# Splitting two weight quads in one operation: a float32 decoder trunk on one core

## The chip, the cores and the metric

One core of one Trainium2 chip. The metric is the device time of one execution in microseconds (us), as the median of several runs; lower is better. Engines: TensorE (PE: matmuls; PEld: its weight loads), VectorE (DVE), ScalarE (ACT), GpSimd (POOL), SyncE (SP: issues the DMAs).

## The reference, cut to what matters

A two-layer decoder trunk on 256 tokens of width 2048, all in float32. The first layer mixes tokens by causal pooling and memory attention, the second by differential attention over shared keys and values and memory attention. After each mixer stands the feed-forward part, width 8192, where the change is:

```python
def squared_relu_mlp(h, w1, w2):
    z = jax.nn.relu(h @ w1)
    return (z * z) @ w2
...
        x = x + squared_relu_mlp(rms_norm(x, ffn_norm[i]), w_ff1[i], w_ff2[i])
```

## The kernel before, in words

**Precision.** Every float32 operand is split in two: `hi`, the value rounded to the type float32r by a cast, and `lo`, the rest, `x - hi`, again in float32r. A product of two operands is hi x hi + hi x lo + lo x hi, all summed in PSUM. The activations are kept as such pairs. The weights come from memory as plain float32 and are split on the chip, just before use.

**The weights' way (class `Feed`, class `Plan`).** The host lays out all weights as 725 rows of 128 x 1024, in the order of use. A row holds eight blocks of 128 x 128; four neighbouring blocks, 512 columns, are a **quad**, so a row is two quads. `Feed.load` (L125) issues one DMA a row on SyncE into one of four buffers `raw`. `Feed._split` (L159) makes the pair: line 164 casts on ScalarE into `hi_ring`, line 165 subtracts on VectorE into `lo_ring`. Both rings have **six slots** of 512 columns. `_slots(n)` hands out n neighbouring slots, the next in turn; where fewer than n are left before the end it starts again at slot 0 and the slots at the end are left out of that round. A slot is free again when the matmuls of its quad have been recorded (`used`, `free`), and its next cast then waits on the chip for the last matmul that reads it.

`Plan` records in a dry run which quads and slab pieces will be used, in order. `Feed.fill` (L210), called when a quad is first used, prepares all splits up to three pieces ahead (`AHEAD`); where no slot is free it stops and goes on at the next call. `Feed._prepare` (L172) prepares one piece. After recording, a scheduler puts the instructions of each engine in the order in which they are then issued; each engine keeps to its order.

**Matmuls with a quad (`a_part`).** A tile of 128 output columns takes 16 blocks. For two blocks at a time, two matmuls of 512 columns multiply `hi` with both parts of the activations, and two of 256 columns multiply `lo` with their high part. A quad is eight matmuls. `hi` and `lo` are the stationary operand: the wait for a split stands at the weight load. In the feed-forward parts the tile's bank is `x_bank`, of which there is one; ScalarE copies it out (line 739, the eviction) before the next tile may begin, and VectorE and ScalarE turn it into squared activations (`z`, and sums of blocks of z, `sit`) for an **up tile** (first matrix), or VectorE adds it to the residual for a **down tile** (second matrix, output columns 0 to 1023).

**Products (`slab_jobs`, `product`).** Columns 1024 to 2047 of the second matrix are computed by seven products of blocks instead of eight, into seven banks p1 to p7 (numbered p0 to p6 in the program). Each 256 x 1024 piece of that matrix is a **slab** of two rows. VectorE forms sums of its four blocks (lines 187 to 197), and the slab is split in four pieces: two slots (for p0 and p1), one (p2), two (p3, p4), two (p5, p6). A product is three matmuls of 512 columns, two with `hi` and one with `lo` (lines 813 to 815). Here `hi` and `lo` are the moving operand.

**The order around the change (`ffn`).** After four up tiles and the opening of the seven banks come 12 up tiles, then three rounds of 24 tiles (8 down, 16 up); with each tile go one or two pieces of a slab, six, nine or six product matmuls at a tile's beginning, a slab in three tiles. So three tiles take six weight rows and one slab. A last part (`last`) does the last eight down tiles and the rest of the slabs. Both layers do the same.

Of the kernel before, what the change touches and what calls it, by code (L numbers as in the profile page):

```python
# [10 lines left out]
F32 = mybir.dt.float32  # L11
# [43 lines left out]
class Plan:  # L55
# [7 lines left out]
    def __init__(self):  # L63
        self.entries = []
        self.npos = 0
        self.jobs = []
        self.slabs = []
# [37 lines left out]
class Feed:  # L105


    def __init__(self, tc, wst, wpool, rows, plan, dry):
        self.tc, self.nc, self.wst, self.wpool, self.rows = tc, tc.nc, wst, wpool, rows
        self.plan, self.dry = plan, dry  # L110
        self.pos = 0
        self.slab_no = 0
        self.lp = self.pp = 0
        self.raw = {}
        self.split = {}
        self.t1 = None
        self.behind = None
        self.gate = None
        if not dry:
            self.hi = wpool.tile([P, SLOTS * 512], F32R, name="hi_ring")  # L120
            self.lo = wpool.tile([P, SLOTS * 512], F32R, name="lo_ring")
            self.busy = [False] * SLOTS
            self.at = 0
# [48 lines left out]
    def _prepare(self, p):  # L172
        sub, add = self.nc.vector.tensor_sub, self.nc.vector.tensor_add
        self.load(self.plan.need[p] + 1 + LOADS)
        if p[0] == "N":
            r = ("N", p[1] // 2)
            c = p[1] % 2 * 512
            if not self._split(p, self.raw[r][:, c : c + 512], 1):
                return False
            if c:  # L180
                del self.raw[r]
            return True
        ra, rb = self.raw[("S", p[1], 0)], self.raw.get(("S", p[1], 1))
        t1 = self.t1[1 if p[1] % 32 > 28 else p[1] % 2]

        def both():
            t2 = rb[:, 0:512].unsqueeze(1).to_broadcast([P, 2, 512])
            two = ra.rearrange("p (a c) -> p a c", a=2)
            sub(two, t2, two)

        if p[0] in "KL":
            one = add(t1, ra[:, 0:512], rb[:, 0:512])
            if self.gate:

                self.order(one, self.gate)
                self.gate = None
            sub(rb[:, 0:512], t1, rb[:, 512:1024])
            if p[0] == "L":
                both()
            return True  # L200
        src, n = ((ra, 2), (t1, 1), (rb, 2), (ra, 2))[p[2]]
        if not self._split(p, src, n):
            return False
        if p[2] == 0 and ("K", p[1]) in self.plan.need:
            both()
        if p[2] == 3:
            del self.raw[("S", p[1], 0)], self.raw[("S", p[1], 1)]
        return True
# [68 lines left out]
def program(ctx, tc, plan, dry, xT, memT, par, lam, cst, wst, yT):  # L277
# [8 lines left out]
    feed = Feed(tc, wst, wp, tp, plan, dry)  # L286
# [10 lines left out]
    def tick():  # L297
        now[0] += 1
        for _, fn in sorted(pend.pop(now[0], []), key=lambda x: x[0]):
            fn()  # L300
# [9 lines left out]
    def mmt(name):  # L310
        return pp.tile([P, 512], F32, tag="mm", bufs=3, name=name)
# [403 lines left out]
    def ffn(l, xs, tags, done):  # L715
# [16 lines left out]
        r = []  # L732
# [40 lines left out]
        def up_tile(q, i, ps):  # L773
            a_part(ps, "w_ff1", l, q * NK + i, range(NK), xs)
            if not r:
                r.append(rstd_from("x"))
            y = evict(ps)

            def first():
                nc.vector.tensor_add(y[:, 0:T], y[:, 0:T], y[:, T : 2 * T])  # L780
                stt(y[:, 0:T], y[:, 0:T], 0.0, r[0], ALU.max, ALU.mult)

            at(1, first)
            at(3, lambda: nc.scalar.activation(stage[i % 8], y[:, 0:T], AF.Square))  # L784
            if q == 0 or i > 0:
                convert(i, 3)
# [19 lines left out]
        def bank():  # L806
            return pp.tile([P, 512], F32, tag="st", bufs=1, name="x_bank")

        def product(p, q, i, a, hi, lo):

            ps = banks[p]
            first, last = q == 0 and i == 0, q == 3 and i == 7
            nc.tensor.matmul(ps, a[1], hi, start=first, stop=False)  # L813
            nc.tensor.matmul(ps, a[0], hi, start=False, stop=False)  # L814
            nc.tensor.matmul(ps, a[0], lo, start=False, stop=last)  # L815

        def slab_jobs(q, i):
            k = q * NK + 2 * i
            n = feed.slab(
                [[("w_ff2", l, k, c, 4), ("w_ff2", l, k + 1, c, 4)] for c in (2, 3)]  # L820
            )

            def plain(c, t):
                return (
                    z[:, 2 * i + c, t * P : t * P + P],
                    z[:, 2 * i + c, T + t * P : T + t * P + P],
                )

            def summed(c):
                return sit[:, i, c * P : c * P + P], sit[:, i, 512 + c * P : 512 + c * P + P]  # L830

            sides = (
                ((0, lambda: plain(0, 0)), (1, lambda: plain(1, 0))),
                ((2, lambda: summed(0)),),
                ((3, lambda: summed(1)), (4, lambda: summed(3))),
                ((5, lambda: summed(2)), (6, lambda: plain(1, 1))),
            )

            def run(j):
                hi, lo = feed.job(n, j)  # L840
                for c, (p, a) in enumerate(sides[j]):
                    s = slice(512 * c, 512 * c + 512)
                    product(p, q, i, a(), hi[:, s], lo[:, s])
                feed.job_used(n, j)

            return run

        def open_banks():
            tags = (("mm", 3), ("mm", 3), ("mm", 3), ("s", 2), ("s", 2), ("o", 1), ("t", 1))
            for p, (tag, bufs) in enumerate(tags):  # L850
                banks.append(pp.tile([P, 512], F32, tag=tag, bufs=bufs, name=f"p{p}"))

        def finish_banks():

            p1, p2, p5, p6, p3, p7, p4 = banks
            low = tp.tile([P, 2, 512], F32, tag="rows", bufs=3, name="c_a")
            upp = tp.tile([P, 2, 512], F32, tag="rows", bufs=3, name="c_b")
            c11, c12 = upp[:, 0, :], upp[:, 1, :]
            u, v = low[:, 0, :], low[:, 1, :]
            add, sub = nc.vector.tensor_add, nc.vector.tensor_sub  # L860
            nc.scalar.copy(u, p1)
            nc.scalar.copy(v, p5)
            add(c11, u, p2)
            add(u, u, p6)
            sub(c12, v, u)
            add(u, u, p7)
            add(c12, c12, p3)
            sub(v, v, u)
            sub(u, u, p4)

            def turn(h):
                c = 8 + 2 * h
                t4 = pp.tile([P, 2, T], F32, tag="ot"[h % 2], bufs=1, name="ct")
                for e in range(2):
                    n = (2 * h + e) // 4
                    w = (2 * h + e) % 4 * P
                    for t, side in enumerate((upp, low)):
                        nc.tensor.transpose(t4[:, e, t * P : t * P + P], side[:, n, w : w + P], ident)
                nc.vector.tensor_add(resid[:, c : c + 2, :], resid[:, c : c + 2, :], t4)
                done(c)  # L880
                done(c + 1)

            for h in range(4):
                at(8 + h // 2 * 2, lambda h=h: turn(h))

        groups = ((0,), (1, 2), (3,))
        for i in range(4):
            up_tile(0, i, mmt("ff1"))
        open_banks()

        for t in range(12):
            if t % 3 == 0:
# [21 lines left out]
        )  # L914

        def last(q=3):
            jobs = [(i, j) for i in range(4, 8) for j in range(4)]
            now_at = []

            def some(n):  # L920
                for _ in range(n):
                    i, j = jobs.pop(0)
                    if j == 0:
                        now_at[:] = [slab_jobs(q, i)]
                    now_at[0](j)
                    tick()

            def between(n):
                return lambda b: some(ends[n][b // 4]) if b > 0 and b % 4 == 0 else None

            for n in range(8):
                if n < 6:
                    some(ends[n][0])
                if n == 5:
                    finish_banks()
                ps = bank() if n < 6 else mmt("ff2")
                down_tile(q, n, ps, between(n) if n < 6 else None)
# [79 lines left out]
    for i in range(2):  # L1017
        c = slice(2 * i, 2 * i + 2)
# [34 lines left out]
    for i in range(2):  # L1053
        c = slice(2 * i, 2 * i + 2)
# [183 lines left out]
    for t in range(2):  # L1238
        four = "p (h d) -> p h d"
        hi, v4 = mv1[:, t, :].rearrange(four, h=4), ps[t].rearrange(four, h=4)  # L1240
        split_rows(hi, mv1_lo[:, :, t, :], v4, mem_c[0][:, t : t + 1])
    for i in range(2):
        c = slice(2 * i, 2 * i + 2)
# [114 lines left out]
    for c in range(3):  # L1358
# [5 lines left out]
        for i in range(2):  # L1364
            j = 2 * c + i
# [119 lines left out]
```

## Time and profile before

| | |
|---|---|
| median of 3 runs | 2032.11 us (2031.99 to 2032.57) |
| the profiled execution: its own time, taken as its span | 2030.2 us |
| feed-forward of the first layer, about | 250 to 930 us of the span |
| feed-forward of the second layer, about | 1340 to 2020 us |
| three tiles with their slab | 21.4 us |

Page 1 of the profile gives each engine's busy time; page 4 follows the chain of work that ended last back from the end; page 5 lists groups of instructions as line, engine, operation, output<-inputs, shapes, count | busy us, mean ns of one | idle time in front and what ended it. In a timeline a row is start, duration, engine, line, operation, and in brackets the idle time in front with what released it; "x2" merges two in a row. A list of waits has the waiting line, the one waited for, total us, times and longest. A row of stretches gives the window, then busy us and (count) for PE, PEld, DVE, ACT and POOL, the granted clock of TensorE, the DMA share and GB/s.

### The profile page before, as it was taken

How to read it: one execution, taken by the hardware profiler on the slowest of the kernel's cores; microseconds unless marked ns; L12 is line 12 of the kernel's file. 1: busy time of each engine (PE TensorE's matmuls, PEld its weight loads, DVE VectorE, ACT ScalarE, POOL GpSimd, SP SyncE). 2: the span in 40 equal slices, each digit the busy share in tenths (PEclk: the TensorE clock that was granted, in tenths of full speed). 3: DMA queues.
4: the chain of work that ended last, by engine and by line, in shares of the span. 5: the costliest groups of instructions: out<-in, count | busy, mean ns of one | idle time of the engine just before them, and what ended most of it. 6: DMA issues, size and time to landing. Idle time of an engine off the chain costs nothing.

```text
span 2030.2 us, 32210 instructions
## 1 busy us (share of the span) xinstructions
PE 2025.3 (100%) x11022; PEld 1744.0 (86%) x11022; DVE 1718.6 (85%) x3233; ACT 1352.6 (67%) x2537; POOL 53.5 (3%) x67
## 2 busy tenths in 40 slices
PE   9999999999999999999999999999999999999999
PEld 8888888888888888888888888888888888888888
DVE  8888889889879978999765798989879978888997
ACT  7765577666656756678665698566657656766764
POOL 0001300000000000000000000310000000000000
PEclk9999999999999999999999999999999999999999
DMA  9566556555556565655565534555555555565564
GB/s 318 167 201 190 191 176 204 191 197 198 187 198 203 185 205 195 206 178 178 187 235 191 173 122 155 188 180 200 187 198 198 187 204 194 188 213 195 193 209 135
DMA packets 110470, 390.75 MB, mean 192 GB/s; under 512 B 12512, under 2 KB 15200, under 8 KB 110304
## 3 DMA queue, kind: packets, MB, share of 16 engines
q1 hardware_dynamic: 110160, 388.68, 57.2%
q8 instruction: 86, 1.41, 0.3%
q14 instruction: 80, 0.66, 0.1%
q10 hardware_dynamic: 144, 0.01, 0.0%
HBM read 386.54 MB, written 2.10 MB: 191 GB/s over the span
## 4 chain that ended last, share of the span: by engine, by line
PE 99%; ACT 0%; DVE 0%; issue 0%
PE x_bank L418 33%; PE x_bank L420 16%; PE wo L418 6%; PE p L813 5%; PE p L814 5%; PE p L815 5%; PE wo L420 3%; PE u L418 2%; PE ff L418 2%; PE u L420 1%; PE q L452 1%; PE q L454 1%; PE k L452 1%; PE q L453 1%; PE k L454 1%; PE v L454 1%
## 5 line engine op out<-in xcount | busy, mean ns | idle before, releaser
L164 ACT CAST hi_ring<-raw 128x512 fp32r<-128x512 f32 x1193 | 736.0, 620 | 510.8 <-PE x_bank L418 302.9
L165 DVE TENSOR_TENSOR lo_ring<-raw,hi_ring 128x512 fp32r<-128x512 f32 x1193 | 816.2, 694 | 189.0 <-ACT hi_ring L164 148.9
L418 PE MATMUL x_bank<-fx,hi_ring 128*128 128x512 f32 x1920 | 601.8, 395 | 0.0
L420 PEld LDWEIGHTS x_bank<-fx,lo_ring 128*128 128x128 f32 x1920 | 360.6, 188 | 84.0
L420 PE MATMUL x_bank<-fx,lo_ring 128*128 128x256 f32 x1920 | 377.1, 278 | 0.0
L418 PEld LDWEIGHTS x_bank<-fx,hi_ring 128*128 128x128 f32 x1920 | 301.3, 189 | 9.4
L418 PE MATMUL x_bank<-z,hi_ring 128*128 128x512 f32 x960 | 300.9, 395 | 0.0
L165 DVE TENSOR_TENSOR lo_ring<-slab,hi_ring 128x1024 fp32r<-128x1024 f32 x188 | 229.9, 1223 | 54.2 <-ACT hi_ring L164 53.5
L164 ACT CAST hi_ring<-slab 128x1024 fp32r<-128x1024 f32 x188 | 196.8, 1047 | 73.3 <-PE x_bank L418 37.8
L420 PEld LDWEIGHTS x_bank<-z,lo_ring 128*128 128x128 f32 x960 | 180.3, 188 | 41.9
L420 PE MATMUL x_bank<-z,lo_ring 128*128 128x256 f32 x960 | 188.6, 278 | 0.0
L418 PE MATMUL wo<-cat,hi_ring 128*128 128x512 f32 x512 | 161.8, 397 | 0.3 <-DVE rc L389 0.3
L418 PEld LDWEIGHTS x_bank<-z,hi_ring 128*128 128x128 f32 x960 | 151.8, 189 | 6.4 <-ACT room L739 0.4
L420 PEld LDWEIGHTS wo<-cat,lo_ring 128*128 128x128 f32 x512 | 95.9, 188 | 22.0
L739 ACT COPY room<-x_bank 128x512 f32<-128x512 f32 x180 | 104.8, 582 | 2.0 <-PE x_bank L420 2.0
L420 PE MATMUL wo<-cat,lo_ring 128*128 128x256 f32 x512 | 101.5, 279 | 0.0
L813 PE MATMUL p<-hi_ring,sit 128*128 128x512 f32 x256 | 100.4, 392 | 0.0
L814 PE MATMUL p<-hi_ring,sit 128*128 128x512 f32 x256 | 100.1, 391 | 0.0
L815 PE MATMUL p<-lo_ring,sit 128*128 128x512 f32 x256 | 99.6, 389 | 0.0
L784 ACT ACTIVATE room<-room 128x256 f32<-128x256 f32 x128 | 53.2, 416 | 42.1 <-DVE room L314 41.9
L418 PEld LDWEIGHTS wo<-cat,hi_ring 128*128 128x128 f32 x512 | 78.3, 189 | 1.1 <-ACT mq L606 0.5
L813 PE MATMUL p<-hi_ring,z 128*128 128x512 f32 x192 | 75.1, 391 | 0.0
(343 smaller groups left out, 3078.2 us busy)
## 6 DMA issues: line engine op xcount, KB each, us to landing
raw<-in_w SPq DMA_DIRECT2D x596, 512.0 KB, 3.7
slab<-in_w SPq DMA_DIRECT2D x124, 512.0 KB, 3.6
memraw<-in_mem SPq DMA_DIRECT2D x5, 512.0 KB, 3.8
resid<-in_x SPq DMA_DIRECT2D x8, 256.0 KB, 5.6
room<-in_w SPq DMA_DIRECT2D x4, 512.0 KB, 5.0
out_y<-resid SPq DMA_DIRECT2D x16, 128.0 KB, 1.9
memraw<-in_mem SPq DMA_DIRECT2D x5, 256.0 KB, 5.6
memraw<-in_mem SPq DMA_DIRECT2D x2, 128.0 KB, 3.6
```

The source lines that it names most:

```text
L164: self.last_cast = self.nc.scalar.copy(hi, src)
L165: low = self.nc.vector.tensor_sub(lo, src, hi.bitcast(F32))
L418: nc.tensor.matmul(ps, hi, xs[:, k, :], start=first and c == 0, stop=False)
L420: nc.tensor.matmul(ps[:, T : 2 * T], lo, xs[:, k, 0:T], start=False, stop=last and c == len(ks) - 1,)
L452: nc.tensor.matmul(ps[t], x[t][1], hi, start=k == 0, stop=False)
L453: nc.tensor.matmul(ps[t], x[t][0], hi, start=False, stop=False)
L454: nc.tensor.matmul(ps[t], x[t][0], lo, start=False, stop=k == NK - 1)
L739: nc.scalar.copy(x, ps)
L784: at(3, lambda: nc.scalar.activation(stage[i % 8], y[:, 0:T], AF.Square))
L813: nc.tensor.matmul(ps, a[1], hi, start=first, stop=False)
L814: nc.tensor.matmul(ps, a[0], hi, start=False, stop=False)
L815: nc.tensor.matmul(ps, a[0], lo, start=False, stop=last)
```

## The change

A flag `pairs` is set when the seven banks are open and cleared at the start of `last`. While it is set, `_prepare` splits both quads of a row at once: it takes two neighbouring slots, casts 1024 columns with one instruction on ScalarE (line 187 of the changed file) and subtracts 1024 columns with one on VectorE (line 188). Each quad is still used and freed by itself. Slab pieces, and weight rows elsewhere, are split as before.

```diff
@@ class Feed, __init__
         self.gate = None
+        self.pairs = False
...
@@ def _prepare(self, p)
         if p[0] == "N":
+            if p in self.split:
+                return True
             r = ("N", p[1] // 2)
             c = p[1] % 2 * 512
+            if c == 0 and self.pairs and ("N", p[1] + 1) in self.plan.need:
+                a = self._slots(2)
+                if a is None:
+                    return False
+                t = self.raw.pop(r)
+                hi, lo = self.hi[:, a * 512 : a * 512 + 1024], self.lo[:, a * 512 : a * 512 + 1024]
+                self.nc.scalar.copy(hi, t)
+                self.nc.vector.tensor_sub(lo, t, hi.bitcast(F32))
+                for j in range(2):
+                    s = slice(512 * j, 512 * j + 512)
+                    self.split[("N", p[1] + j)] = (hi[:, s], lo[:, s], range(a + j, a + j + 1))
+                return True
             if not self._split(p, self.raw[r][:, c : c + 512], 1):
                 return False
...
@@ def ffn
         open_banks()
+        feed.pairs = True
...
         def last(q=3):
+            feed.pairs = False
             jobs = [(i, j) for i in range(4, 8) for j in range(4)]
```

## The prediction

> **What bounds the kernel now.** I read the page first: busy shares, the clock line of the slices, and the chain that ended last.
>
> ```profile
> span 2030.2 us, 32210 instructions
> ...
> PE 2025.3 (100%) x11022; PEld 1744.0 (86%) x11022; DVE 1718.6 (85%) x3233; ACT 1352.6 (67%) x2537; POOL 53.5 (3%) x67
> ...
> PEclk9999999999999999999999999999999999999999
> ...
> PE 99%; ACT 0%; DVE 0%; issue 0%
> ```
>
> The chain runs on TensorE for 99% of the span, at full granted clock. A busy TensorE alone could hide slow matmuls, so the waits come next: who waits for the splits, and whether TensorE ever does.
>
> ```profile
> PEld x_bank L418 <- ACT room L739: 0.4, 2, 0.2
> ...
> PEld mk L445 <- ACT hi_ring L164: 0.3, 1, 0.3
> ```
>
> ```profile
> ACT hi_ring L164 <- PE x_bank L418: 343.8, 489, 2.0
> DVE lo_ring L165 <- ACT hi_ring L164: 203.2, 364, 1.9
> ```
>
> In the first two rows TensorE's weight loads wait for a split once, 0.3 us, at the start. In the other two the splits wait: ScalarE's cast 489 times for TensorE to give a slot of the ring back, VectorE's subtraction 364 times for the cast. So the splits run ahead of TensorE, and what holds them is the ring of six slots, not either engine. Time on ScalarE or VectorE is worth nothing here; how far ahead they run is worth everything.
>
> **What the change does to the engines.** The groups of operations give both shapes, since slabs are split 1024 wide already.
>
> ```profile
> L164 ACT CAST hi_ring<-raw 128x512 fp32r<-128x512 f32 x1193 | 736.0, 620 | 510.8 <-PE x_bank L418 302.9
> L165 DVE TENSOR_TENSOR lo_ring<-raw,hi_ring 128x512 fp32r<-128x512 f32 x1193 | 816.2, 694 | 189.0 <-ACT hi_ring L164 148.9
> ...
> L165 DVE TENSOR_TENSOR lo_ring<-slab,hi_ring 128x1024 fp32r<-128x1024 f32 x188 | 229.9, 1223 | 54.2 <-ACT hi_ring L164 53.5
> L164 ACT CAST hi_ring<-slab 128x1024 fp32r<-128x1024 f32 x188 | 196.8, 1047 | 73.3 <-PE x_bank L418 37.8
> ```
>
> The changed kernel has 334 casts and 334 subtractions fewer, so 334 pairs (167 a layer). A pair costs ScalarE 1047 ns instead of 2 x 620, VectorE 1223 instead of 2 x 694: 334 x 193 ns = 64 us and 334 x 165 ns = 55 us less busy. Both leave idle engines idler: I count 0.
>
> What it takes away is lead. A pair needs two free neighbouring slots; at slot 5 it skips to slot 0 and leaves one unused; the cast waits until both are given back; and the first quad is ready only after 1.05 + 1.22 us instead of 0.62 + 0.69. I followed each slot through the order of both kernels' instructions: the matmul time between the last read of a slot and the first read of its next contents. Before, the shortest is 3.7 us for the high part and most are 5.1 to 5.8. After, most row pairs have 3.0 to 4.4, and twice in every three slabs (64 us) come places with 0.9 to 1.9. Per layer, place B comes 9 times and place C 8 times: 18 and 16 in all. On SyncE's queue row and slab loads only change places with their neighbours; a row's load follows a pair's subtraction, still three rows (8 us of matmuls) ahead, so I count the DMAs at nothing.
>
> **The prices of one hand-over**, from the timeline. Cadence and release:
>
> ```profile
> 503.46 0.39 PE L815 MATMUL p<-lo_ring,sit 128*128 128x512 f32 x1
> 503.68 0.39 PE L813 MATMUL p<-hi_ring,z 128*128 128x512 f32 x1
> ...
> 507.84 0.63 PE L418 MATMUL x_bank<-fx,hi_ring 128*128 128x512 f32 x2
> 508.31 0.39 PE L420 MATMUL x_bank<-fx,lo_ring 128*128 128x256 f32 x2
> 508.53 0.62 PE L418 MATMUL x_bank<-fx,hi_ring 128*128 128x512 f32 x2
> ```
>
> ```profile
> 508.50 0.62 ACT L164 CAST hi_ring<-raw 128x512 fp32r<-128x512 f32 x1 [0.77 <-PE x_bank L418]
> ```
>
> ```profile
> 505.42 1.23 DVE L165 TENSOR_TENSOR lo_ring<-slab,hi_ring 128x1024 fp32r<-128x1024 f32 x1 [0.31 <-ACT hi_ring L164]
> ...
> 508.03 1.89 DVE L165 TENSOR_TENSOR lo_ring<-raw,hi_ring 128x512 fp32r<-128x512 f32 x3
> ```
>
> ```profile
> 504.34 1.05 ACT L164 CAST hi_ring<-slab 128x1024 fp32r<-128x1024 f32 x1 [0.26 <-PE p L814]
> ```
>
> A product matmul takes 0.228 us, two blocks (two high, two low matmuls) 0.695, so a quad 1.39. The second high matmul started at 507.84 + 0.235; the cast it released began at 508.50, 0.43 later. The subtraction starts 0.03 after its cast (504.34 + 1.05 = 505.39). Back to back, operations overlap by 0.08 (three of 0.685 in 1.89).
>
> How late a stalled TensorE restarts, and how early an eviction by an idle ScalarE starts:
>
> ```profile
> 267.82 0.40 PE L420 MATMUL ff<-fx,lo_ring 128*128 128x256 f32 x2
> ...
> 268.26 0.59 ACT L739 COPY room<-ff 128x512 f32<-128x512 f32 x1 [0.48 <-PE ff L420]
> ```
>
> ```profile
> 904.35 0.58 ACT L739 COPY room<-x_bank 128x512 f32<-128x512 f32 x1
> ...
> 904.98 0.30 PEld L418 LDWEIGHTS x_bank<-z,hi_ring 128*128 128x128 f32 x2 [0.22 <-ACT room L739]
> ...
> 905.55 0.40 PE L420 MATMUL x_bank<-z,lo_ring 128*128 128x256 f32 x2
> ```
>
> The second low matmul started at 267.94; the eviction 0.32 after it. At 904.93 an eviction ended, the weight load began at 904.98, and the low matmuls came at 905.55, where 0.465 after the first high one is usual: the high matmul in effect ran from 905.09, 0.16 after the release. I take 0.16 as restart; 0.05 (weight load alone) is the lower bound, a lower operation queued in front (0.4) the upper.
>
> **Place C, walked through** (zero: first of the four products after a tile; order: p3 high twice, p4 high twice, p3 low, p4 low, one quad, p5 high twice, p6 high, p5 low, p6 high, two high matmuls of the next quad, p6 low, its lows). The slab piece in slots 0, 1 was cast from -1.42 to -0.37 and subtracted from -0.34 to 0.88. p3 low wants it at 0.91 and gets it at 0.88 + 0.16 = 1.04: **0.13 lost**. The next slab piece goes into the same slots when p4's second high matmul (0.68) gives them back: cast 1.11 to 2.16, subtracted 2.19 to 3.41, in time for p5 low at 3.57. The row pair in slots 2, 3 follows the quad's last high matmul (2.43): cast 2.86 to 3.91, high wanted at 4.03, had at 4.07: **0.04**. Its subtraction, 3.94 to 5.16, lets the low matmuls start at 5.32 instead of 4.76: **0.56**. Sum 0.73 behind down tiles. Behind up tiles VectorE has the tile's two operations in front, 0.42 us each by these rows,
>
> ```profile
> L314 DVE SCALAR_TENSOR_TENSOR room<-room,r_x 128x256 f32<-128x256 f32 x128 | 53.8, 420 | 0.7
> L780 DVE TENSOR_TENSOR room<-room 128x256 f32<-128x256 f32 x128 | 53.5, 418 | 1.2 <-ACT room L739 1.2
> ```
>
> and the same walk gives 0.96: the tile's last row pair is 0.11 late, p3 low 0.25, then 0.04 and 0.56 as before. With two thirds up tiles I take 0.9: 16 x 0.9 = 14.4 us.
>
> **Place B** (zero: first of nine products after a tile; then one quad, p5 and p6 high, a high pair of a new row, p5 and p6 low, p0 high of the next slab). Three 1024-wide fills want the engines at once: a row cast 1.34 to 2.39, a slab piece 2.30 to 3.35, and the row needed first, whose slots come free last (2.98), 3.41 to 4.46. p5 high: 3.51 instead of 3.44 (**0.07**). The row's high pair: 4.62 instead of 4.42 (**0.20**). VectorE takes them in that order, to 3.64, 4.78 and 5.92. The next slab's cast needs the second subtraction and runs 4.82 to 5.87, so p0 high comes at 6.03 instead of 5.54 (**0.49**). Sum 0.76, with an up tile's square between 0.80: 18 x 0.8 = 14.4 us.
>
> **Between tiles** the one bank of x_bank must be evicted. Before, six or nine products (1.37 us) cover it. The new order has only four at 82 boundaries: 0.115 + 0.91 = 1.03 us after the last low start, against 0.32 + 0.58 + 0.16 = 1.06: 0.03 each, 2.5 us. At 20 boundaries with seven products a 1024 cast stands right before the eviction: 0.07 each, 1.4 us. Elsewhere a lead of 3.0 us, 3.5 to the first low read, stands against 0.2 + 1.05 + 0.03 + 1.22 + 0.16 = 2.7 us for a hand-over (0.2 is the release counted from the matmul's end); 0.5 to 0.8 are spare.
>
> Sum: 14.4 + 14.4 + 2.5 + 1.4 = 32.7 us. On the profiled 2030.2 that is 2062.9; the median of the runs, 2032.1, lies 1.9 above, so **2064.8**, say 2065.
>
> The Trainium skill, "Perfetto Trace Analysis", section Optimizing Scalar/DVE Operations, has a rule on each side: group operations "if the engine is saturated", and where Scalar and Vector are not saturated but cause bubbles elsewhere, break instructions up. By the rows above neither is saturated, so its second rule speaks against this change, and the walks agree; its first rule is rival 2.
>
> **Rivals.** (1) *VectorE falls behind.* Its busiest stretches leave little:
>
> ```profile
> 600.00:700.00 100.00, 100.00 (x547) 86.24 (x546) 90.66 (x164) 69.86 (x123) 0.00 (x0) 1.00 0.60 200
> ...
> 1200.00:1300.00 100.00, 99.25 (x649) 88.16 (x648) 89.07 (x263) 79.84 (x239) 13.38 (x15) 1.00 0.47 153
> ```
>
> At 90.7% busy, with lead halved, two further 0.42 us operations ahead of a subtraction use up the spare of a 3.0 us fill. About 90 such fills (45 a layer) at 0.5 us more make 45 us: 2110. For it: the share. Against: my walk found them in time. Chance 0.17. The second row has 0.75 us of idle TensorE with clock 1.00, so short stalls cost only themselves.
> (2) *The grouping itself pays: faster.* If VectorE were the bound between tiles, the 55 us would come off: 1977; half, 2005. It decides as soon as TensorE waits for subtractions before the change. The two rows of TensorE's own waits above name a cast and an eviction, no subtraction. Chance 0.03.
> (3) *No change, 2032.* The matmuls that the new order pulls forward cover the holes, if TensorE's restart costs nothing and releases come 0.3 earlier. Against: in C cast and subtraction alone take 1.05 + 1.22 = 2.27 us, and 2.06 lie between release and first low read. Chance 0.05.
> (4) *It doesn't do what it says*: the pairs fail to form. The 334 missing operations in the new order exclude it; chance 0.
>
> **Numbers.** My forecast, slower by 11 to 60 us, 0.75. With restart 0.05 the places lose about 0.1 at each of six steps: 10 us less, and boundaries 4 less, 2050; I go below that to 2043, since the 82 boundaries are so even that 0.1 us either way in each is 8 us. Rival 1 sets the upper end, 2110. A measurement tells about 0.2% (4 us) from no change; slower 0.92, same 0.05, faster 0.03.
>
> **What would show it.** In the new page 334 casts and subtractions `<-raw` 128x1024 near 1047 and 1223 ns and 525 casts of 512; TensorE below 100% with some 30 us of waits for the pairs' subtraction (lo_ring) and cast (hi_ring), in two clusters per 64 us, the longest near 0.56; clock 1.00. Wrong if TensorE's waits spread over all fills (rival 1), or if they mostly name the eviction.

## The result, and the profile after

The changed kernel takes **2077.19 us** (median of 4 runs, 2074.55 to 2078.57) against 2032.14 (4 runs, 2031.99 to 2032.57): a ratio of 1.022, 95% interval 1.0205 to 1.0234. It is slower, as forecast, and the time lies in the range; the forecast 2065 is 12 us short. The profiled execution has a span of 2076.8 us, 46.6 more than before, where the sum had 32.7.

The page of the changed kernel, first lines and the chain that ended last:

```profile
span 2076.8 us, 31025 instructions
...
PE 2058.5 (99%) x11022; PEld 1728.6 (83%) x11022; DVE 1698.2 (82%) x2899; ACT 1311.0 (63%) x2203; POOL 53.5 (3%) x67
...
PE 91%; DVE 4%; ACT 3%; DMA 1%; issue 1%; DVEq 0%; ACTq 0%
```

The chain no longer stays on TensorE: 8% of it runs over VectorE, ScalarE and DMA. The granted clock is 1.00 in both feed-forward parts, and nearly all of the loss is there. From the start of its first matmul to the start of the last one into `x_bank`, each of the two parts took 676.7 us before and takes 700.3 and 699.5 after: 23.6 and 22.8 us more, of 46.6.

The groups of the two new operations and of the casts that are left (line, engine, operation, shapes, count | busy, mean ns | idle time in front and its releasers):

```profile
L188 DVE TENSOR_TENSOR lo_ring<-raw,hi_ring 128x1024 fp32r<-128x1024 f32 x334 | 406.7, 1222 | 140.2 <-ACT hi_ring L187 137.5 <-PE x_bank L435 1.0
L187 ACT CAST hi_ring<-raw 128x1024 fp32r<-128x1024 f32 x334 | 348.9, 1050 | 249.1 <-PE x_bank L433 204.7 <-DVE lo_ring L166 17.5 <-DMA raw<-in_w 11.7
L165 ACT CAST hi_ring<-raw 128x512 fp32r<-128x512 f32 x525 | 321.4, 620 | 210.9 <-DVE lo_ring L166 59.6 <-PE wo L433 56.1 <-PE u L433 17.4
```

Counts and durations are those expected. The waits of TensorE's weight loads (us in total, times, longest):

```profile
PEld x_bank L435 <- DVE lo_ring L188: 24.4, 42, 1.2
PEld x_bank L433 <- ACT room L754: 19.3, 102, 0.2
PEld x_bank L433 <- ACT hi_ring L187: 12.9, 36, 0.7
PEld p L828 <- ACT hi_ring L165: 11.8, 20, 0.7
PEld p L830 <- DVE lo_ring L166: 9.1, 25, 1.0
```

Before, this list named one eviction line with 0.4 us and one cast with 0.3. Now it names both pair operations, the slab pieces and the eviction. A weight load runs ahead of its matmuls, so its idle time isn't TensorE's loss: the 102 waits for the eviction are 0.19 us each, and the matmuls behind them come 0.04 to 0.07 late. And what is new among ScalarE's waits (the first row is from the kernel before, the others from the changed one):

```profile
ACT room L739 <- PE x_bank L420: 2.0, 2, 1.0
...
ACT room L754 <- PE x_bank L435: 106.8, 138, 2.0
ACT hi_ring L187 <- DMA raw<-in_w: 11.7, 13, 2.3
```

Before, ScalarE stood at an eviction of `x_bank` twice for the end of a tile; now 138 times, up to 2.0 us, with all its later work queued behind. And 13 pairs wait for their row's DMA.

**Place B** in the changed kernel's timeline (start, duration, engine, line, operation; "x2" merges two in a row, so a late second one shows as a longer duration):

```profile
552.53 0.46 PE L828 MATMUL p<-hi_ring,sit 128*128 128x512 f32 x1
552.83 0.39 PE L829 MATMUL p<-hi_ring,sit 128*128 128x512 f32 x1
...
553.28 0.39 PE L829 MATMUL p<-hi_ring,z 128*128 128x512 f32 x1
553.75 0.73 PE L433 MATMUL x_bank<-z,hi_ring 128*128 128x512 f32 x2
554.31 0.39 PE L830 MATMUL p<-lo_ring,sit 128*128 128x512 f32 x1
554.54 0.40 PE L830 MATMUL p<-lo_ring,z 128*128 128x512 f32 x1
555.07 0.50 PE L828 MATMUL p<-hi_ring,z 128*128 128x512 f32 x1
555.40 0.40 PE L435 MATMUL x_bank<-z,lo_ring 128*128 128x256 f32 x2
```

At 0.228 us a matmul, the second row comes 0.07 late, the row's high pair 0.24, its second matmul 0.10 (0.73 for the two instead of 0.63), the next slab's first product 0.30 and the matmul behind it 0.10: about 0.82 us, where the walk had 0.07 + 0.20 + 0.49.

**Place C**, again the changed kernel's timeline:

```profile
506.16 0.40 PE L829 MATMUL p<-hi_ring,sit 128*128 128x512 f32 x1
506.50 0.73 PE L830 MATMUL p<-lo_ring,sit 128*128 128x512 f32 x2
...
509.53 1.22 DVE L188 TENSOR_TENSOR lo_ring<-raw,hi_ring 128x1024 fp32r<-128x1024 f32 x1
...
510.11 0.40 PE L830 MATMUL p<-lo_ring,z 128*128 128x512 f32 x1
510.81 0.51 PE L435 MATMUL x_bank<-fx,lo_ring 128*128 128x256 f32 x2 [0.30 <-DVE lo_ring L188]
```

p3's low matmul is 0.11 late and the next another 0.11; the row's low matmul comes 0.70 after the one before it instead of 0.23, right after its subtraction ended (509.53 + 1.22 = 510.75), and the next 0.11 more. The 0.47 + 0.11 are the 0.56 of the walk.

**What the walk did not have** stands in the same timeline:

```profile
1671.82 0.33 SPq L138 DMA_DIRECT2D raw<-in_w  x1
...
1676.80 2.00 ACT L187 CAST hi_ring<-raw 128x1024 fp32r<-128x1024 f32 x2 [2.32 <-DMA raw<-in_w]
1677.88 2.36 DVE L188 TENSOR_TENSOR lo_ring<-raw,hi_ring 128x1024 fp32r<-128x1024 f32 x2 [2.48 <-ACT hi_ring L187]
...
1680.29 0.30 PEld L435 LDWEIGHTS x_bank<-z,lo_ring 128*128 128x128 f32 x2 [1.15 <-DVE lo_ring L188]
```

ScalarE stands 2.32 us for a row whose load SyncE had issued at 1671.82. Two pairs then follow each other without a gap, and the low matmul waits for the second subtraction. So the cast that waits is not that of the row TensorE needs next. By the semaphores that the casts wait for, each of the 13 casts that wait for a DMA belongs to a row two further on in the order of use, which stands in front in ScalarE's queue; the cast behind it is that of the row needed first, and that row had landed long before (here at 1667.8). The late row itself was needed only at 1688.9, when TensorE reached it. Ten of the 13 loads took 3.1 to 3.4 us from issue to landing, and no idle gap of TensorE over 0.15 us follows within 6 us; the other three took 4.7 to 5.5 us, and behind them TensorE lost 3.7 us.

### The profile page after: what moved, and what is told of

The parts are those of the page before. It is cut to its first block, busy times and chain, and to the rows that moved or that the text cites. A ratio compares the mean times of both kernels' runs of the same rounds, so it can differ in the third digit from the quotient of the medians.

```text
span 2076.8 us, 31025 instructions
## 1 busy us (share of the span) xinstructions
PE 2058.5 (99%) x11022; PEld 1728.6 (83%) x11022; DVE 1698.2 (82%) x2899; ACT 1311.0 (63%) x2203; POOL 53.5 (3%) x67
## 4 chain that ended last, share of the span: by engine, by line
PE 91%; DVE 4%; ACT 3%; DMA 1%; issue 1%; DVEq 0%; ACTq 0%
PE x_bank L433 29%; PE x_bank L435 15%; PE wo L433 6%; PE p L828 4%; PE p L829 4%; PE p L830 4%; PE wo L435 3%; PE u L433 2%; PE ff L433 2%; DVE lo_ring L188 2%; DVE lo_ring L166 2%; ACT hi_ring L165 1%; PE u L435 1%; PE q L467 1%; PE k L467 1%; PE q L469 1%
## 5 line engine op out<-in xcount | busy, mean ns | idle before, releaser
L188 DVE TENSOR_TENSOR lo_ring<-raw,hi_ring 128x1024 fp32r<-128x1024 f32 x334 | 406.7, 1222 | 140.2 <-ACT hi_ring L187 137.5
L187 ACT CAST hi_ring<-raw 128x1024 fp32r<-128x1024 f32 x334 | 348.9, 1050 | 249.1 <-PE x_bank L433 204.7
L165 ACT CAST hi_ring<-raw 128x512 fp32r<-128x512 f32 x525 | 321.4, 620 | 210.9 <-DVE lo_ring L166 59.6
L166 DVE TENSOR_TENSOR lo_ring<-raw,hi_ring 128x512 fp32r<-128x512 f32 x525 | 363.0, 702 | 106.6 <-ACT hi_ring L165 95.8
L435 PE MATMUL x_bank<-fx,lo_ring 128*128 128x256 f32 x1920 | 381.5, 280 | 5.3 <-DVE lo_ring L188 5.1
L433 PEld LDWEIGHTS x_bank<-fx,hi_ring 128*128 128x128 f32 x1920 | 295.8, 189 | 27.4 <-ACT room L754 13.6
```

What stands on the lines that cost most here:

```text
L165: self.last_cast = self.nc.scalar.copy(hi, src)
L166: low = self.nc.vector.tensor_sub(lo, src, hi.bitcast(F32))
L187: self.nc.scalar.copy(hi, t)
L188: self.nc.vector.tensor_sub(lo, t, hi.bitcast(F32))
L433: nc.tensor.matmul(ps, hi, xs[:, k, :], start=first and c == 0, stop=False)
L435: nc.tensor.matmul(ps[:, T : 2 * T], lo, xs[:, k, 0:T], start=False, stop=last and c == len(ks) - 1,)
```

## Experiments

**Theory.** What is lost is lead: TensorE stalls where the time between the last read of a slot and the first read of its new contents is shorter than a hand-over, and a hand-over of a pair is long. **Rival A:** not the width but the bookkeeping costs (slots taken in pairs, skipped slots, products moved). **Rival B:** each wide operation costs by its own length, wherever it stands (46.6 us / 334). **Rival C:** loads and engine load. **Rival D:** one engine's half is to blame. The column "parts" is the time of the two feed-forward parts, taken as above, over the 676.7 us each of before, from the traces.

| kernel | median us | ratio to before (95%) | parts, us |
|---|---|---|---|
| changed | 2077.2 | 1.022 (1.0205 to 1.0234) | +23.6, +22.8 |
| narrow in pairs | 2043.7 | 1.0055 (1.004 to 1.007) | +5.0, +5.8 |
| seven slots, three row buffers | 2058.1 | 1.0125 (1.011 to 1.0141) | +5.4, +15.8 |
| three row buffers | 2077.7 | 1.0224 (1.0209 to 1.0239) | +20.9, +22.2 |
| before, four slots | 2078.9 | 1.0228 (1.0211 to 1.0245) | +23.1, +24.5 |
| narrow at B and C | 2082.1 | 1.0246 (1.023 to 1.0261) | +24.6, +26.2 |
| narrow at two others | 2078.8 | 1.0229 (1.0214 to 1.0244) | +25.7, +21.8 |
| no skip | 2064.0 | 1.016 (1.0143 to 1.0177) | +15.5, +15.5 |
| wide cast only | 2070.4 | 1.0189 (1.0173 to 1.0204) | +18.4, +21.1 |
| seven slots, no slab difference | 2045.8 | 1.0062 (1.0047 to 1.0077) | 0.0, +9.3 |
| changed, no slab difference | 2074.2 | 1.0207 (1.0191 to 1.0222) | +21.7, +20.4 |
| wide subtraction only | 2095.4 | 1.0311 (1.0295 to 1.0326) | +28.4, +35.8 |
| before, seven slots, three row buffers | 2039.1 | 1.0035 (1.0024 to 1.0046) | +1.8, +0.4 |

### Narrow operations in pair slots

```diff
-                self.nc.scalar.copy(hi, t)
-                self.nc.vector.tensor_sub(lo, t, hi.bitcast(F32))
+                for h in range(2):
+                    c2 = slice(512 * h, 512 * h + 512)
+                    self.nc.scalar.copy(hi[:, c2], t[:, c2])
+                    self.nc.vector.tensor_sub(lo[:, c2], t[:, c2], hi[:, c2].bitcast(F32))
```

> The two slots of a row are still taken together and the sixth slot is still skipped, but each quad has its own cast and its own subtraction of 512 columns again. Theory (lost lead: stalls come only where release to first read is shorter than a hand-over): a narrow hand-over needs about 0.98 us to the high part and 1.70 us to the low part, and by the order of the instructions only 22 fills miss that, by 2.3 us in all; 2034 to 2040 us. Rival A (the ring's bookkeeping, skipped slots and the moved products alone make the loss): stays at 2065 to 2078 us. Rival B (each 1024 operation costs TensorE something by its own length): 2032 us, since none is left.

2043.7 us, 4 us above the theory's range. With the same pairs of slots and the same skips, 33 of the 45 us go when the operations are narrow again: the width is most of the loss, and rival A alone is excluded. But 11 us stay with no wide row operation left. They are A's share, or short leads that a narrow hand-over misses too, since the slots are as in the changed kernel; this run doesn't part the two. The waits of the weight loads:

```profile
PEld x_bank L437 <- DVE lo_ring L190: 9.7, 25, 0.5
PEld x_bank L435 <- ACT room L756: 6.6, 27, 0.3
```

They are short and many, none over 0.5 us.

### Seven slots, and two controls

Three constants are changed: slots, rows loaded ahead and row buffers; the row buffers pay for the seventh slot. The first control has the fewer row buffers and six slots, the second is the kernel before with all three constants.

```diff
-SLOTS, AHEAD, LOADS, KOFF, RAWS = 6, 3, 3, 2, 4
+SLOTS, AHEAD, LOADS, KOFF, RAWS = 7, 3, 2, 2, 3
```

> The changed kernel with seven slots in both rings instead of six, and three raw buffers with two rows loaded ahead instead of four and three, to make room. All 334 wide casts and subtractions stay. Theory (lost lead): the shortest lead is 3.0 us to the high part where 1.41 are needed and 3.0 to 3.5 to the low part where 2.64 are needed; one fill misses by 0.1 us; 2032 to 2042 us. Rival B (every wide operation costs by itself, 46.6 us / 334 = 0.14 us each): unchanged, about 2077 us. Rival C (VectorE or ScalarE too busy between tiles): also nearly unchanged, since their work is the same.

> The changed kernel with six slots and three raw buffers with two rows loaded ahead: the control for the seven-slot kernel. Every theory of the rings: 2074 to 2082 us. If it came near 2040, fewer row buffers and not the seventh slot would be what helps there; if it were above 2090, the loads would be late.

> The kernel before with seven slots and three raw buffers: control for the two kernels with seven slots. All theories but C: 2031 to 2034 us. Rival C (two rows loaded ahead are too few): 2050 us or more.

The row buffers alone change nothing after the change (2077.7), so the seventh slot brings 19.6 us; what the feed-forward parts lose falls from 43.1 to 21.2. That excludes rival B: the 334 wide operations are all there. But 2058 is 16 us above the theory's range, with leads of 3.0 us and more. The control without pairs costs 7.0 us, only 2.2 of it in these parts (the first begins 6.9 us later), so the loads alone don't explain the 21.2 either. The ring's lead is not the whole of it. The seven-slot kernel's timeline shows the rest:

```profile
1452.20 1.05 ACT L187 CAST hi_ring<-raw 128x1024 fp32r<-128x1024 f32 x1
1452.72 0.42 DVE L761 TENSOR_TENSOR z<-room,z 128x256 fp32r<-128x256 f32 x1
1453.05 1.22 DVE L204 TENSOR_TENSOR slab<-slab,slab 128x1024 f32<-128x1024 f32 x1
...
1454.19 1.22 DVE L188 TENSOR_TENSOR lo_ring<-raw,hi_ring 128x1024 fp32r<-128x1024 f32 x1
...
1455.46 0.50 PE L435 MATMUL x_bank<-fx,lo_ring 128*128 128x256 f32 x2 [0.55 <-DVE lo_ring L188]
```

The cast ended at 1453.25, and no slot was missing; but VectorE had begun the slab's difference at 1453.05, and the pair's subtraction started 0.94 us after its cast. TensorE lost 0.7 us. A wide subtraction delivers both quads only at its end, so a wide operation in front of it counts in full.

### The slab difference left out

```diff
             t2 = rb[:, 0:512].unsqueeze(1).to_broadcast([P, 2, 512])
             two = ra.rearrange("p (a c) -> p a c", a=2)
+            return
             sub(two, t2, two)
```

The `return` leaves out VectorE's 1024-wide difference once a slab, so these kernels compute something else; they are for the time alone.

> The changed kernel with seven slots and three raw buffers, and without VectorE's 1024-wide slab difference (1.22 us, once a slab); the last two block differences of each slab are left out of the computation. The seven-slot kernel lost 26 us although the ring no longer held anything up; all its stalls of over 0.15 us in the second feed-forward part are low matmuls of x_bank. Theory (two terms: lost lead, and wide subtractions that stand in VectorE's queue behind another wide operation): both are gone; 2032 to 2038 us. Rival B (each of the 334 wide operations costs by its length): 2058 us, nothing changes. Rival C (the third raw buffer is missed): 2055 to 2060 us.

> The changed kernel, six slots, without the same slab difference; the same part of the computation is left out. Theory (lost lead is the first term, VectorE's queue the second): with six slots the fills are late because their slots come back late, so VectorE's spare time brings little: 2070 to 2076 us. If VectorE alone were the bound (rival 1 of the prediction), it would come down as the seven-slot kernel does, by 20 us or more, to 2055 us or below.

With seven slots 12.3 us go (2058.1 to 2045.8), and the first feed-forward part loses nothing any more: 0.0 us, with all its wide row operations in place. So there the two terms, slots and VectorE's time in front of a subtraction, are the whole loss; whether it is the place in the queue or the 1.22 us of work itself was not parted. With six slots the same edit brings 3.0 us, in the range expected: there the slots come back too late for VectorE's spare time to help, and rival 1 of the prediction is not what bounds the changed kernel. The 9.3 us that stay in the second part are above the theory's range. The seven-slot kernel without the difference, timeline of its longest stall:

```profile
1746.10 1.05 ACT L187 CAST hi_ring<-raw 128x1024 fp32r<-128x1024 f32 x1 [0.34 <-PE x_bank L434]
1747.47 0.69 DVE L208 TENSOR_TENSOR room<-slab,slab 128x512 f32<-128x512 f32 x1 [2.51 <-DMA slab<-in_w]
1748.08 0.42 DVE L762 TENSOR_TENSOR z<-room,z 128x256 fp32r<-128x256 f32 x1
1748.42 1.22 DVE L188 TENSOR_TENSOR lo_ring<-raw,hi_ring 128x1024 fp32r<-128x1024 f32 x1
...
1749.69 0.50 PE L436 MATMUL x_bank<-fx,lo_ring 128*128 128x256 f32 x2 [1.53 <-DVE lo_ring L188]
```

VectorE stood 2.51 us at a slab sum whose DMA had not landed, with the pair's subtraction behind it. Such waits take 20.0 us (26 times) in the second part and 0.6 us (twice) in the first. Why the slabs come late in one part and not in the other was not tried.

### Four slots in the kernel before

```diff
-SLOTS, AHEAD, LOADS, KOFF, RAWS = 6, 3, 3, 2, 4
+SLOTS, AHEAD, LOADS, KOFF, RAWS = 4, 3, 3, 2, 4
```

> The kernel before, no wide row operation at all, with four slots in both rings instead of six. Theory (lost lead): leads of 0.5 to 1.5 us at about 50 fills a layer where a narrow hand-over needs 0.98 and 1.70; 118 fills miss by 60 us taken one by one, against 59 us by the same count in the changed kernel, which lost 46.6; so about 2065 to 2090 us. Rival B (loss in proportion to the wide row operations): 2032 us. Rival A (skips and moved products): 2035 to 2050 us, the products before a tile stay six or more.

2078.9 us, inside the theory's range and outside those of A and B: without any wide row operation, lost slots alone cost as much as the change. Nearly all of it is in the feed-forward parts here too (23.1 + 24.5 us).

### Narrow at places B and C, and at two others

```diff
-            if c == 0 and self.pairs and ("N", p[1] + 1) in self.plan.need:
+            if c == 0 and self.pairs and self.k % 18 not in (1, 7) and ("N", p[1] + 1) in self.plan.need:
```

The counter k numbers the rows since the flag was set; the control has 4 and 10 in place of 1 and 7. A row that is narrow here also takes its two slots one at a time, as in the kernel before.

> The changed kernel with 38 of the 334 rows split in narrow operations again: the two rows in 18 that stand at places B and C. Theory (lost lead at places): in place C the two late steps of the row go (about 0.6 us x 18), in place B the late high pair and part of the last step (0.35 to 0.6 us x 20): 18 to 25 us come back, 2050 to 2060 us. Rival B (0.14 us for each wide operation): 38 x 0.14 = 5 us come back, 2072 us.

> The control: 38 other rows are narrow again, two in 18 with the common lead of 3.0 us. Theory (lost lead at places): nothing comes back but a few of the small waits, 2074 to 2078 us. Rival B: 5 us come back, 2072 us. If it came back as much as with the rows of B and C, the loss is spread over all fills and not tied to places.

In the control nothing comes back, as expected (2078.8, 0.8 us above its range). The first does not: 2082.1, where 2050 to 2060 was expected. Its weight loads wait for other things:

```profile
PEld x_bank L436 <- ACT room L757: 30.3, 70, 1.3
PEld x_bank L438 <- DVE lo_ring L190: 28.0, 60, 2.1
PEld p L831 <- ACT hi_ring L166: 8.3, 18, 0.5
```

The waits for the slab's high pieces fall, those for the eviction go from 0.2 to 1.3 us at the longest. One of them in the timeline of this kernel:

```profile
549.50 0.62 ACT L777 CAST sit<-room 128x512 fp32r<-128x512 f32 x1 [1.02 <-DVE room L774]
550.03 1.04 ACT L189 CAST hi_ring<-raw 128x1024 fp32r<-128x1024 f32 x1
550.98 0.57 ACT L757 COPY room<-x_bank 128x512 f32<-128x512 f32 x1
...
551.61 0.73 PE L436 MATMUL x_bank<-z,hi_ring 128*128 128x512 f32 x2 [0.82 <-ACT room L757]
```

The tile ended at 549.7. Its eviction stood third in ScalarE's queue, behind a cast that waited 1.02 us for VectorE and a pair's cast of 1.04. So my picture of two faulty rows was too narrow: the order of both queues is made anew around any edit, and the lateness shows wherever it is next needed. The prices of B and C are real; that they can be taken out one by one is not.

### No skipped slot

```diff
-            if c == 0 and self.pairs and ("N", p[1] + 1) in self.plan.need:
+            if c == 0 and self.pairs and self.at < SLOTS - 1 and ("N", p[1] + 1) in self.plan.need:
```

> The changed kernel, but where the next slot is the last of the ring the row is split in narrow operations instead of leaving that slot unused: 266 of the 334 wide pairs stay. Theory (lost lead): 52 fills miss by 13.5 us taken one by one, against 134 by 59 us in the changed kernel; 2040 to 2052 us. Rival B: 266 x 0.14 = 37 us stay, 2069 us.

2064.0 us: 13 of the 45 us go with 68 of 334 pairs, somewhat more than rival B's share (68 x 0.14 = 9.5) and 12 us short of the theory. By itself it does not decide between them; in the feed-forward parts 31.0 us stay of 46.5.

### One engine's half alone

In the first, the two narrow subtractions of "narrow in pairs" with the wide cast; in the second its two narrow casts with the wide subtraction.

> The row's cast stays 1024 wide on ScalarE, its subtraction is two of 512 again; slots are taken in pairs. Theory (lost lead, the low part is what comes last): the low part needs 0.2 + 1.05 + 0.03 + 0.69 + 0.16 = 2.13 us instead of 2.64, so the 0.56 of place C goes and the late steps of B that wait for a high part stay; 2045 to 2060 us. Rival D (ScalarE's wide cast delays evictions and slab casts and is the cause): about 2077 us.

> The mirror of the wide cast alone: two casts of 512 on ScalarE, one subtraction of 1024 on VectorE, slots in pairs. Theory (the low part comes last, and a wide subtraction starts only after the second cast and delivers both quads at its end): the first quad's low part needs 0.2 + 1.16 + 0.03 + 1.22 + 0.16 = 2.77 us, more than with both wide (2.64), and ScalarE has 64 us more to do: 2076 to 2095 us. If the wide cast were the harm: below 2055 us.

2070.4 us with the wide cast alone, 10 us above the range expected; 2095.4 with the wide subtraction alone, just above its range. The subtraction is the worse half, but the halves don't add: 38 and 63 us alone, 45 together. The waits of the weight loads, first for the wide cast alone:

```profile
PEld x_bank L435 <- ACT room L756: 26.5, 96, 0.6
PEld p L832 <- DVE lo_ring L166: 13.8, 42, 1.3
```

and for the wide subtraction alone:

```profile
PEld x_bank L435 <- ACT room L756: 30.3, 78, 0.7
PEld p L832 <- DVE lo_ring L166: 26.0, 39, 1.9
```

In both, the slab's low pieces (line 166) wait more than in the changed kernel (9.1 us): they stand behind row operations in VectorE's queue. With the wide subtraction alone they wait up to 1.9 us.

No kernel here beats the one before: TensorE is busy there for 2025.3 of 2030.2 us, so there is little to win on the way of the weights.

## Why the prediction was right, and where it was short

**What bounds the kernel: right.** ScalarE is busy for 41.6 us less and VectorE for 20.4 us less, and the kernel is 45 us slower. (64 and 55 had been worked out from counts. The durations add up to 63.3 and 51.7 us less; the page counts the time in which an operation overlaps the next only once.)

**The mechanism: right.** Lead for the wide hand-over is what is lost: a seventh slot gives 19.6 us back, four slots in the kernel before cost as much as the change. The Trainium skill, "Perfetto Trace Analysis", section Optimizing Scalar/DVE Operations, says that breaking instructions up may let work finish sooner where Scalar and Vector are not saturated but cause bubbles on other engines; the runs agree: the same slots with narrow operations take 33.5 us off.

**The terms of the sum.** For each matmul I took the time to the next one's start less what it takes undisturbed, and added it up by place:

| term | predicted | measured |
|---|---|---|
| place B | 18 x 0.8 = 14.4 | 20 x 0.82 = 16.4 |
| place C | 16 x 0.9 = 14.4 | 18 x 0.83 = 14.9 (mostly 0.76, up to 1.06) |
| behind a DMA that lands late | 0 | 5.2 in six stalls of 0.7 to 1.0: four at rows (3.7), two at slabs (1.5) |
| behind another wide operation, elsewhere | 0 | 0.9 in two stalls |
| starts of tiles behind four products | 82 x 0.03 = 2.5 | 0.04 each, about 3 |
| starts behind seven products | 20 x 0.07 = 1.4 | 20 x 0.07, about 1.5 |
| the rest | 0 | about 5, most about 0.1 a piece |

B and C were priced to within a tenth and counted one too few in each layer. The term of the seven products is as foretold, with a 1024 cast right before the eviction and 0.70 us for two high matmuls instead of 0.63:

```profile
527.66 1.05 ACT L187 CAST hi_ring<-raw 128x1024 fp32r<-128x1024 f32 x1 [1.49 <-PE x_bank L433]
...
528.62 0.58 ACT L754 COPY room<-x_bank 128x512 f32<-128x512 f32 x1
...
529.29 0.70 PE L433 MATMUL x_bank<-fx,hi_ring 128*128 128x512 f32 x2
```

The step that failed is "so I count the DMAs at nothing". The loads were early enough for TensorE (the one shown was issued 17 us before its row was needed), but a row's cast could stand two rows ahead of its turn in ScalarE's queue and wait there for its DMA, with the row needed next behind it. That, and two slabs for which VectorE waited 1.6 and 1.3 us with a subtraction behind, cost 5.2 us. Late slabs are not new: VectorE waited 12.3 us for them before, 24 times, and TensorE never stood still for it. That "0.5 to 0.8 are spare" elsewhere failed in part as well: with a slab's difference in front, a 3.0 us fill is a little late. No term of the sum stands for these stalls and the rest, 11 us in all; that 2077 lies in the range all the same is owed to the range's width. The restart at 0.16 held, in two pieces (below).

**What would show it.** The pairs' subtraction and cast make 37.3 of the waits named above, against the 30 foretold; the longest is 1.2 and not 0.56, since late rows come on top. The eviction is named most often, which I had called a sign of being wrong; it isn't, since those waits cost 0.04 to 0.07 us each.

**The rivals.** VectorE falling behind (0.17) is a second term and not the bound: taking 1.22 us a slab off it brings 3.0 us with six slots and 12.3 with seven. The row of 90.7% was not its busiest: in 800 to 900 us of the kernel before it is busy for 92.7%. The grouping paid nowhere; no change is excluded. (Against no change, the walk itself has 4.76 - 2.86 = 1.90 us from the cast's start to the first low read, not 2.06; the argument holds the better.)

**Open:** why the two halves don't add, and why the rows at B and C can't be mended alone, was read from their queues and not tested; an order of ScalarE's and VectorE's instructions fixed by hand, with the rows' casts in the order of use, was not tried.

## What to carry to other kernels

An engine that is often idle can still be the one whose latency counts: before joining two operations, compare the joined operation's whole hand-over (release, both operations, restart) with the shortest lead that the buffers leave, and ask in whose queue something must stand behind it. A joined operation takes its buffers later and gives its result later, and what stands behind it in the queue is late with it; look also for operations that stand in front of their turn and wait for a DMA. Where the lead was short, a slot gave back 19.6 us and less work for VectorE 3.0, and mending the places where the stall showed only moved it.

## What the runs showed of the hardware that was not expected

- A restart of TensorE costs in two pieces. After place C's subtraction ended (510.75) the weight load and the first matmul came at 510.81, 0.06 later; the second matmul then came 0.11 late (0.51 for the two low matmuls instead of 0.40, and 0.73 for two high ones at 553.75 instead of 0.63).
- Waits of the weight loads for evictions, 19.3 us in all, cost TensorE 4 to 5 us (82 x 0.04 + 20 x 0.07), since the loads run ahead of the matmuls.
